# Taking ScalarE out of the row sums of six steps, and its align directive with it

## The chip, the cores and the metric

The kernel runs on one core of one Trainium2 chip. The metric is the device time of one execution in microseconds; for the kernel before, it is the median of three runs.

## The reference

For each of 8 batches, the reference multiplies a 4096x512 matrix `x` by the transpose of a 4096x512 matrix `y`, but keeps only the diagonal of the product, and takes a softmax over it. So only the row-by-row dot products of `x` and `y` are wanted:

```python
gram = np.matmul(x, y.transpose(0, 2, 1))        # B, N, D = 8, 4096, 512, all float32
diag = np.diagonal(gram, axis1=1, axis2=2)
diag = diag - diag.max(axis=-1, keepdims=True)
exp = np.exp(diag)
return (exp / exp.sum(axis=-1, keepdims=True)).astype(np.float32)
```

There are 32768 dot products of length 512. The inputs are 134.22 MB, the output is 0.13 MB.

## The kernel before, in words

TensorE is not used. The rows are laid over the 128 partitions, and each partition works through `R = 32` rows per step; there are eight steps, and four of them make one half of the output (four batches). One step takes in 8.39 MB of `x` and as much of `y`. There are two buffers for `x`, `xs[0]` and `xs[1]`, used in turn, and a single buffer `ys` for `y`. All loads are issued on one queue, that of SyncE (SP), in the order x, y, x, y.

The first six steps (t = 0 to 5) are the same, and are the ones that the change touches. VectorE (DVE) multiplies the first 26 rows of `xs` in place by `ys` (`products`, line 72). In the meantime ScalarE (ACT) copies the last `K = 6` rows of `ys` into a tile `side` (line 126), so that VectorE can multiply these rows from `side` and `ys` comes free earlier. As soon as both have read `ys`, SP issues the `y` load of the next step (line 68). Then the 512 products of each row are summed: VectorE reduces the first 30 rows in one instruction (`sums`, line 75), and ScalarE sums the last `W = 2` rows, each with an activation that has an accumulator as second output (`sums_act`, line 80). When both are done with this `xs` buffer, SP issues the `x` load of the step after the next into it (line 65). After the fourth step the softmax of the first half follows (`exps` and `normalize`, lines 93 to 113).

Step 6 and step 7 are written out differently. In step 6 ScalarE sums 30 rows, VectorE two. Step 7 loads in small pieces, and VectorE multiplies and sums each row in one instruction (`dots`, line 85), so that little is left to do after the last piece has landed. Then the softmax of the second half follows, and its result is stored from ScalarE's queue (line 169).

There is no scheduler: the order on each engine is that of the source, and the waits follow from which tile is read and written. Ahead of the loop stand one align directive for VectorE (line 117) and one for ScalarE (line 118). Such a directive asks that the next instruction of that engine be placed at a multiple of 128 instruction slots. In the trace each is one branch on its engine's queue, of 47 ns and 33 ns. Two drains of SP (lines 120 and 121) stand between them and the first load.

Of the kernel before, what the change touches and what calls it, by code (L numbers as in the profile page):

```python
# [1 line left out]

# [5 lines left out]


@with_exitstack
def kernel(
    ctx: ExitStack,
    tc: tile.TileContext,
    x: bass.AP,
    y: bass.AP,
    out: bass.AP,
):
    nc = tc.nc
    ctx.enter_context(tc.manual_schedule())  # L20
    f32 = mybir.dt.float32
    Alu = mybir.AluOpType
    Act = mybir.ActivationFunctionType
    X = mybir.AxisListType.X
    B, N, D = x.shape
    P = nc.NUM_PARTITIONS
    G = 32
    Q = P // G
    C = N // G
    R = 32  # L30
    H = R // 2
    K = 6
    W = 2
    F = H + 1
    L = 9
    S = B // Q * (C // R)


    xv = x.rearrange("(s b) (j c) d -> s (b j) c d", b=Q, j=G)
    yv = y.rearrange("(s b) (j c) d -> s (b j) c d", b=Q, j=G)  # L40
    ov = out.rearrange("(s b) (j c) -> s (b j) c", b=Q, j=G)

    big = ctx.enter_context(tc.tile_pool(name="big", bufs=1))
    small = ctx.enter_context(tc.tile_pool(name="small", bufs=1))


    xs = [big.tile([P, R, D], f32, name=f"xs{i}") for i in range(2)]
    ys = big.tile([P, R, D], f32, name="ys")
    side = big.tile([P, K, D], f32, name="side")

    diag = [small.tile([P, C + 2 * i], f32, name=f"diag{i}") for i in range(B // Q)]
    res = [small.tile([P, C], f32, name=f"res{i}") for i in range(B // Q)]

    def columns(t, r0, n):
        c0 = t % (C // R) * R + r0
        return slice(c0, c0 + n)

    def rows(t, r0, n):
        return xs[t % 2][:, r0 : r0 + n, :]

    def dots_of(t, r0, n):
        return diag[t * R // C][:, columns(t, r0, n)]

    def load_x(t, r0, n):
        nc.sync.dma_start(out=rows(t, r0, n), in_=xv[t * R // C, :, columns(t, r0, n), :])  # L65

    def load_y(t, r0, n):
        nc.sync.dma_start(out=ys[:, r0 : r0 + n, :], in_=yv[t * R // C, :, columns(t, r0, n), :])  # L68

    def products(t, r0, n, yt):  # L70
        xt = rows(t, r0, n)
        nc.vector.tensor_tensor(out=xt, in0=xt, in1=yt, op=Alu.mult)  # L72

    def sums(t, r0, n):
        nc.vector.tensor_reduce(out=dots_of(t, r0, n), in_=rows(t, r0, n), axis=X, op=Alu.add)  # L75

    def sums_act(t, r0, n):
        for r in range(r0, r0 + n):
            row = xs[t % 2][:, r, :]
            nc.scalar.activation(out=row, in_=row, func=Act.Copy, accum_out=dots_of(t, r, 1))  # L80

    def dots(t, r0, n):
        for r in range(r0, r0 + n):
            xt = xs[t % 2][:, r, :]
            nc.vector.scalar_tensor_tensor(  # L85
                out=xt, in0=xt, scalar=1.0, in1=ys[:, r, :], op0=Alu.mult, op1=Alu.mult,
                accum_out=dots_of(t, r, 1),
            )

    def over_quadrant(name, column, op, negate=False):  # L90

        got = small.tile([P, 1], f32, name=name)
        nc.vector.tensor_reduce(  # L93
            out=got, in_=column.to_broadcast([P, G]), axis=X, op=op, negate=negate, apply_transpose=True
        )
        return got

    def largest(out, d):
        nc.vector.tensor_reduce(out=out, in_=d, axis=X, op=Alu.max)  # L99

    def exps(i, d):
        mxp = small.tile([P, 1], f32, name=f"mxp{i}")
        largest(mxp, d)
        nmx = over_quadrant(f"nmx{i}", mxp, Alu.max, negate=True)
        sump = small.tile([P, 1], f32, name=f"sump{i}")
        nc.scalar.activation(out=res[i], in_=diag[i][:, :C], func=Act.Exp, bias=nmx, scale=1.0, accum_out=sump)  # L106
        return sump

    def normalize(i, sump):
        total = over_quadrant(f"sum{i}", sump, Alu.add)  # L110
        rc = small.tile([P, 1], f32, name=f"rc{i}")
        nc.vector.reciprocal(out=rc, in_=total)  # L112
        nc.vector.tensor_single_scalar(out=res[i], in_=res[i], scalar=rc, op=Alu.mult)  # L113

    nc.vector.addr_align(128, offset=0, max_nops=0)
    nc.scalar.addr_align(128, offset=0, max_nops=0)

    nc.sync.drain()  # L120
    nc.sync.drain()  # L121

    for t in range(S - 2):
        load_x(t, 0, R)
        load_y(t, 0, R)
        nc.scalar.activation(out=side, in_=ys[:, R - K :, :], func=Act.Copy)  # L126
        if t == C // R:
            normalize(0, sump)
        products(t, 0, R - K, ys[:, : R - K, :])
        products(t, R - K, K, side)  # L130
        sums(t, 0, R - W)
        sums_act(t, R - W, W)
        if t == C // R - 1:
            sump = exps(0, diag[0])

    t = S - 2
    load_x(t, 0, R)
    load_y(t, 0, R)
    spare = rows(t + 1, R - L, L)
    nc.scalar.activation(out=spare, in_=ys[:, F - L : F, :], func=Act.Copy)  # L140
    products(t, 0, F - L, ys[:, : F - L, :])
    products(t, F - L, L, spare)
    products(t, F, R - F, ys[:, F:, :])
    sums(t, R - W, W)
    sums_act(t, 0, R - W)
    largest(diag[1][:, C + 1 :], diag[1][:, : C - 2 * R])


    t += 1
    upto = {load_x: 0, load_y: 0}  # L150
    done = 0
    for load, n in (
        (load_x, H - 1), (load_y, F), (load_x, 8), (load_y, 10), (load_x, 6), (load_y, 3), (load_x, 2), (load_y, 2), (load_x, 1)
    ):
        load(t, upto[load], n)
        upto[load] += n
        both = min(upto.values())
        dots(t, done, both - done)
        done = both
        if done == F:  # L160
            largest(diag[1][:, C : C + 1], diag[1][:, C - 2 * R : C - R + H])

    met = small.tile([P, C - R], f32, name="met")
    nc.scalar.activation(out=met, in_=diag[1][:, : C - R], func=Act.Copy)  # L164

    for p in range(0, P, H):
        nc.sync.dma_start(out=ov[0, p : p + H, :], in_=res[0][p : p + H, :])
    normalize(1, exps(1, diag[1][:, C - R + H :]))
    nc.scalar.dma_start(out=ov[1], in_=res[1])


# [1 line left out]
_INS = ['x', 'y']  # L173
_OUTS = [((8, 4096), 'float32')]


# [23 lines left out]
```

## Time and profile before

| what | value |
|---|---|
| three runs | 320.30, 320.35, 320.43 us; median 320.35 |
| span of the profiled execution | 318.8 us |
| bytes read, mean rate over the span | 134.22 MB, 421 GB/s |
| VectorE busy | 241.7 us (76%), 98 instructions |
| ScalarE busy | 49.8 us (16%), 97 instructions |
| sum over 30 rows (line 75) | 6 of 16.153 us |
| sum over one row on ScalarE (line 80) | 42 of 0.617 us, and 42 reads of the accumulator of 0.187 us |

The page and the trace give the profiled execution its span, from the first to the last instruction, and no other time; the median of the runs is 1.55 us above that span. The busy share of an engine is over the whole span; whether an engine's work sets the end is read from the chain of waits and from the idle time ahead of its instructions.

### The profile page before, as it was taken

Reading aid. Unit: us, or ns where it says so; the run is one execution under the profiler, and the core shown is the slowest. Engines: PE = TensorE matmul, PEld = TensorE weight load, DVE = VectorE, ACT = ScalarE, POOL = GpSimd, SP = SyncE. Lnnn points to the kernel's source line nnn. Section 1 sums busy time; section 2 is a strip of 40 time slices with the busy share of each in tenths; the row PEclk is TensorE's granted clock in tenths of the full one; section 3 lists DMA queues with packets and bytes.
Section 4 is the critical chain, followed back from the end, with each engine's and each line's share of the span. In section 5 each row is a group of like instructions: output and inputs, shape, how many; then the busy total and the mean of one; then the engine's idle time right before and its main releaser. Section 6 shows DMA issues by size and latency. Waiting matters only on the chain.

```text
span 318.8 us, 315 instructions
## 1 busy us (share of the span) xinstructions
DVE 241.7 (76%) x98; ACT 49.8 (16%) x97; POOL 0.2 (0%) x4
## 2 busy tenths in 40 slices
DVE  0000069995899939999399994999939998599996
ACT  1000030100301003010120103000030100596700
POOL 0000000000000000000000000000000000000000
DMA  9999999999999999999999999999999999999993
GB/s 372 419 395 469 452 395 452 469 395 395 493 428 395 469 452 395 428 477 411 395 485 436 395 469 452 395 403 493 419 395 469 452 395 452 394 440 410 429 411 112
DMA packets 3714, 134.37 MB, mean 421 GB/s; under 512 B 512, under 2 KB 768, under 8 KB 1280
## 3 DMA queue, kind: packets, MB, share of 16 engines
q1 hardware_dynamic: 3568, 134.29, 97.7%
q10 hardware_dynamic: 144, 0.07, 0.1%
q14 instruction: 2, 0.02, 0.0%
HBM read 134.22 MB, written 0.13 MB: 421 GB/s over the span
## 4 chain that ended last, share of the span: by engine, by line
DMA 65%; DVE 33%; SPq 1%; issue 0%; ACT 0%; DVEq 0%
DMA ys<-in_y_dram 65%; DVE xs L72 32%; DVE xs L85 0%; SPq L65 0%; SPq L68 0%; DVE res L113 0%; DVE sum L93 0%; DVE nmx L93 0%; ACT res L106 0%; DVE mxp L99 0%; DVE rc L112 0%; DVEq L72 0%; SPq L121 0%; SPq L120 0%
## 5 line engine op out<-in xcount | busy, mean ns | idle before, releaser
L72 DVE TENSOR_TENSOR xs<-xs,ys 128x13312 f32<-128x13312 f32 (+2 forms) x8 | 96.7, 12091 | 71.9 <-DMA ys<-in_y_dram 71.9
L75 DVE TENSOR_REDUCE diag<-xs 128x30 f32<-128x15360 f32 (+1 forms) x7 | 98.1, 14020 | 0.2
L80 ACT ACTIVATE xs<-xs 128x512 f32<-128x512 f32 x42 | 25.9, 617 | 90.4 <-DVE xs L72 90.4
L126 ACT ACTIVATE side<-ys 128x3072 f32<-128x3072 f32 x6 | 16.6, 2763 | 124.1 <-DMA ys<-in_y_dram 124.1
L85 DVE SCALAR_TENSOR_TENSOR xs<-xs,ys 128x512 f32<-128x512 f32 x32 | 19.9, 687 | 1.1 <-DMA ys<-in_y_dram 1.0
L72 DVE TENSOR_TENSOR xs<-xs,side 128x3072 f32<-128x3072 f32 x6 | 20.1, 3351 | 0.0
L80 ACT ACTIVATION_READ_ACCUMULATOR xs<-xs 128x1 f32 x42 | 7.9, 187 | 0.0
L140 ACT ACTIVATE xs<-ys 128x4608 f32<-128x4608 f32 x1 | 4.0, 4043 | 20.0 <-DMA ys<-in_y_dram 20.0
L106 ACT ACTIVATE res<-diag,nmx 128x128 f32<-128x128 f32 x2 | 0.8, 402 | 30.1 <-DVE nmx L93 30.1
L72 DVE TENSOR_TENSOR xs<-xs,xs 128x4608 f32<-128x4608 f32 x1 | 5.0, 4951 | 0.0
L85 DVE DVE_READ_ACCUMULATOR xs<-xs,ys 128x1 f32 x32 | 2.6, 82 | 0.0
L126 ACT ACT_TABLE_LOAD x1 | 1.3, 1283 | 1.2 <-PEq L184 1.2
L93 DVE TRANSPOSE_TENSOR_REDUCE sum<-sump 128x1 f32<-128x32 f32 x2 | 0.4, 212 | 1.2 <-ACT res L106 1.2
L113 DVE TENSOR_SCALAR res<-res,rc 128x128 f32<-128x128 f32 x2 | 0.6, 286 | 0.1
L99 DVE TENSOR_REDUCE mxp<-diag 128x1 f32<-128x128 f32 (+1 forms) x2 | 0.5, 229 | 0.1
L93 DVE TRANSPOSE_TENSOR_REDUCE nmx<-mxp 128x1 f32<-128x32 f32 x2 | 0.4, 211 | 0.1
L99 DVE TENSOR_REDUCE diag<-diag 128x1 f32<-128x64 f32 (+1 forms) x2 | 0.4, 202 | 0.0
L112 DVE RECIPROCAL rc<-sum 128x1 f32<-128x1 f32 x2 | 0.3, 164 | 0.1
L106 ACT ACTIVATION_READ_ACCUMULATOR res<-diag,nmx 128x1 f32 x2 | 0.4, 186 | 0.0
L164 ACT ACTIVATE met<-diag 128x96 f32<-128x96 f32 x1 | 0.3, 283 | 0.0
L184 POOL MEMSET const-bfloat16-1.0<- 128x1 bf16 x1 | 0.1, 102 | 0.0
L184 POOL MEMSET const-uint8-127<- 128x1 uint8 x1 | 0.1, 101 | 0.0
(2 smaller groups left out, 0.2 us busy)
## 6 DMA issues: line engine op xcount, KB each, us to landing
ys<-in_y_dram SPq DMA_DIRECT2D x1, 4352.0 KB, 14.9
xs<-in_x_dram SPq DMA_DIRECT2D x1, 3840.0 KB, 14.2
ys<-in_y_dram SPq DMA_DIRECT2D x1, 2560.0 KB, 12.9
xs<-in_x_dram SPq DMA_DIRECT2D x1, 2048.0 KB, 19.4
xs<-in_x_dram SPq DMA_DIRECT2D x1, 1536.0 KB, 16.3
ys<-in_y_dram SPq DMA_DIRECT2D x1, 768.0 KB, 17.7
xs<-in_x_dram SPq DMA_DIRECT2D x1, 512.0 KB, 18.5
ys<-in_y_dram SPq DMA_DIRECT2D x1, 512.0 KB, 19.3
```

Of the source, the lines that this page charges most:

```text
L72: nc.vector.tensor_tensor(out=xt, in0=xt, in1=yt, op=Alu.mult)
L75: nc.vector.tensor_reduce(out=dots_of(t, r0, n), in_=rows(t, r0, n), axis=X, op=Alu.add)
L80: nc.scalar.activation(out=row, in_=row, func=Act.Copy, accum_out=dots_of(t, r, 1))
L85: nc.vector.scalar_tensor_tensor(out=xt, in0=xt, scalar=1.0, in1=ys[:, r, :], op0=Alu.mult, op1=Alu.mult, accum_out=dots_of(t, r, 1),)
L93: nc.vector.tensor_reduce(out=got, in_=column.to_broadcast([P, G]), axis=X, op=op, negate=negate, apply_transpose=True)
L99: nc.vector.tensor_reduce(out=out, in_=d, axis=X, op=Alu.max)
L106: nc.scalar.activation(out=res[i], in_=diag[i][:, :C], func=Act.Exp, bias=nmx, scale=1.0, accum_out=sump)
L112: nc.vector.reciprocal(out=rc, in_=total)
L113: nc.vector.tensor_single_scalar(out=res[i], in_=res[i], scalar=rc, op=Alu.mult)
L126: nc.scalar.activation(out=side, in_=ys[:, R - K :, :], func=Act.Copy)
L140: nc.scalar.activation(out=spare, in_=ys[:, F - L : F, :], func=Act.Copy)
L164: nc.scalar.activation(out=met, in_=diag[1][:, : C - R], func=Act.Copy)
```

## The change

The align directive of ScalarE (line 118) is taken out; that of VectorE stays. In the six like steps VectorE's reduction takes all 32 rows, and ScalarE's twelve activations with accumulator are gone. `W` is still used in step 6, which is not touched. The wait of five of the `x` loads on ScalarE goes with the activations; their wait on VectorE stays. All lines from 118 on move up by one, those from 131 on by two.

```diff
     nc.vector.addr_align(128, offset=0, max_nops=0)
-    nc.scalar.addr_align(128, offset=0, max_nops=0)
...
         products(t, R - K, K, side)
-        sums(t, 0, R - W)
-        sums_act(t, R - W, W)
+        sums(t, 0, R)
         if t == C // R - 1:
             sump = exps(0, diag[0])
```

## The prediction

> **What bounds the kernel now.** I read the page's slices first, because a kernel that only streams its inputs should show its DMA engines full.
>
> ```profile
> DVE  0000069995899939999399994999939998599996
> ACT  1000030100301003010120103000030100596700
> DMA  9999999999999999999999999999999999999993
> ```
>
> Each digit is a fortieth of the span. The DMA row is at 90% or more from the first slice to the last but one. VectorE has holes in every step, ScalarE is mostly idle. So something that ends earlier or later on VectorE or ScalarE moves the end only if it makes a hole in the DMA row, or if it lies after the last landing.
>
> Second, the chain that ended last, in order of time, for the pitch of the steps:
>
> ```profile
> 56.62 24.50 DMA ys<-in_y_dram
> 81.12 0.03 issue
> ...
> 81.21 14.04 DVE xs L72
> 95.25 0.02 SPq L68
> 95.27 0.03 issue
> 95.30 24.52 DMA ys<-in_y_dram
> ```
>
> The columns are start, length and what. The chain names VectorE's product and the y load in turn, but that is not a VectorE bound: 24.5 us is issue to landing of a load whose bytes take less, since it first queues behind the x load ahead of it. The y loads land at 81.12 and 119.82, 38.70 us apart, and in each interval 16.78 MB come in: 433.5 GB/s. At that rate one load takes 19.35 us. All 134.22 MB need 309.6 us of the 318.8; the rest is the start (the first load is issued at 0.83) and the tail after the last landings (313.24 to 318.8).
>
> Third, the groups of instructions with shapes kept apart, for the prices:
>
> ```profile
> L75 DVE TENSOR_REDUCE diag<-xs 128x30 f32<-128x15360 f32 x6 | 96.9, 16153 | 0.2
> L72 DVE TENSOR_TENSOR xs<-xs,ys 128x13312 f32<-128x13312 f32 x6 | 84.2, 14025 | 66.7 <-DMA ys<-in_y_dram 66.7
> L75 DVE TENSOR_REDUCE diag<-xs 128x2 f32<-128x1024 f32 x1 | 1.2, 1220 | 0.0
> ```
>
> The last columns are busy us, mean ns of one, and idle time of the engine before them with what ended it. The product always waits for y: 42.5 us once at the start, then about 5 us per step.
>
> Fourth, the timeline, for how early the x loads are issued:
>
> ```profile
> 59.83 16.15 DVE L75 TENSOR_REDUCE diag<-xs 128x30 f32<-128x15360 f32 x1
> 60.98 0.19 ACT L80 ACTIVATION_READ_ACCUMULATOR xs<-xs 128x1 f32 x1
> 76.06 0.33 SPq L65 DMA_DIRECT2D xs<-in_x_dram  x1
> 81.21 14.03 DVE L72 TENSOR_TENSOR xs<-xs,ys 128x13312 f32<-128x13312 f32 x1 [5.22 <-DMA ys<-in_y_dram]
> ```
>
> The x load of step 2 goes out at 76.06, right after the reduction (75.98); ScalarE had finished at 61.17. The y load then in flight lands at 81.12. So the next load is in the queue 5.06 us before the one ahead of it has landed. This lead is what the change eats into.
>
> **The change part by part.**
>
> *The longer reduction.* From 1,024 elements (1.220 us) to 15,360 (16.153 us) the slope is 14.933 us over 14,336 elements, 1.042 ns each. Two more rows are 1,024 elements, so +1.067 us: 17.22 us. Six of them are 6.4 us of VectorE time. In a step VectorE then works from 81.21 to about 115.76 instead of 114.69, and its idle time before the next product falls from 5.22 to about 4.15 us. In step 3 the softmax of the first half also follows; its idle time was 3.24 us by the timeline and becomes about 2.2. Idle time remains in every step, so the product still starts on the landing of y, and the y load after it is issued when it was. Cost while this cover holds: 0. Without it: up to 1.07 us a step.
>
> *The later x loads.* Six x loads (steps 2 to 7) are released by these reductions. Each is issued 1.07 us later, at 77.13 for the first, and the lead shrinks from 5.06 to 3.99 us. How much lead is needed the trace does not state, so I bound it. The first load is issued at 0.83, and the DMA share is 0.53 in the window 0 to 2 us and 0.97 in 2 to 4 us: the engines are filled within about 2.5 us of an issue. And the y load of step 7 is issued at 279.27, while the x load ahead of it, issued at 269.63, lands after 14.2 us at 283.8: a lead of 4.6 us that leaves no hole in the DMA row. 3.99 is above 2.5 and a little below 4.6, so it lies outside the leads seen in steady running, but above the need seen at the start. Lower bound 0, upper bound six times 1.07 or 6.4 us; I take 0, by the row at the start, which is the nearest to what is asked (issue to full engines). SP has nothing else to lose: the instruction after the delayed x load is the next y load, which waits for a product that ends 19 us later.
>
> *The removed activations.* Twelve activations of 0.617 us and twelve accumulator reads of 0.187 us. A pair of rows occupies ScalarE from 59.83 to 61.17, 1.34 us, beside a reduction of 16.15 us. Nothing waits for them that does not wait longer for the reduction. ScalarE's next work is the copy at 81.20. Gain: 0. No transfer is removed or added, and steps 6 and 7 and the last softmax are as before, so the tail (313.24 to 318.8) keeps its length.
>
> *The removed directive.* It is one branch of 33 ns at 0.73 us; after it ScalarE loads its table at 1.17 and then waits for y until 42.43. Up to 0.4 us may be saved there under a wait of 40 us: 0. Two other things hang on it. In the stretch from 1 to 3 us the trace has instruction fetches, and nowhere else in the span:
>
> ```profile
> q14 instruction: 2, 0.02, 4.8%
> ```
>
> That is packets, MB and share of 16 engines: two packets of about 8 KB, and 4.8% of 16 engines over 2 us is 1.54 us of DMA engine time, 0.77 us each. They follow the two branches of lines 117 and 118 by about a microsecond. Without ScalarE's branch, one of them should either vanish or be fetched later, when ScalarE's code runs over the next boundary. If it goes, one of 16 DMA engines has up to 0.77 us less to do; the loads land when the slowest engine is done, so the gain is between 0 and 0.77 us. If it comes in mid-run, the same bounds hold as a loss against a start without it, so between a loss of 0.77 and a gain of 0.77 in all. I take 0, because only one engine of 16 is concerned and the window from 2 to 4 us has the others still filling.
>
> The Trainium skill (Runtime: NRT & Kernel Launch, Instruction fetch mechanics) says that an engine's code is fetched ahead in order, block by block, so that running over a boundary is mostly hidden, while a taken branch out of the fetched window stalls the engine. It calls a block 16 KiB; the packets here are of 8 KB. By that rule too the sum would be 0 for the boundary, and a small gain on ScalarE for the branch, under the same 40 us wait.
>
> Sum against the profiled execution: 318.8 + 0, and 1.55 us around it as in the runs before: 320.35 us.
>
> **The rivals.**
>
> *A: all hidden,* as summed: 320.35, give or take 0.3 for small shifts in the landings. For it: full DMA row, 4 us of VectorE idle time left, 40 us of cover for ScalarE. Against it: the lead and the fetch are bounded, not measured.
>
> *B: ScalarE's code is fetched in mid-run (slower).* Place: where ScalarE's unaligned code reaches a boundary, a packet goes between full data queues. Price: 0.77 us if it lands on the DMA engine that finishes last, and 0.40 us more if ScalarE stalls there just before the last exponential (the idle time seen after its branch, 0.77 to 1.17 us). So 320.65 to 321.5. It decides once the packet costs the last engine over 0.64 us. Against it: ScalarE counts 97 instructions before and 73 after, so there is less code to run over a boundary, and most of it has cover.
>
> *C: the lead is too short (slower).* If a load needs more than 3.99 us to fill the engines without a hole, each of six x loads opens one, of up to 1.07 us: 320.35 to 326.8. It decides from a needed lead of about 4.0 us. Against it: 2.5 us sufficed at the start. The Trainium skill (VectorE: DVE Perf Modes, Rules for kernel authors) warns of this direction: it calls the reduction VectorE's slowest operation and advises against it on the hot path. The trace disagrees in part: 1.052 ns per element here against 1.054 for the product.
>
> *D: a lighter start (faster).* One fetch fewer lets the last engine begin and end earlier: down to 320.35 - 0.77, or 319.6.
>
> That the change does not do what it says I can exclude for the sums (the built program has reductions of 32 rows and no such activations); for the directive, the branch in the trace shows that it was more than a remark.
>
> **How the numbers follow.** A measurement of this kernel can tell 0.2%, or 0.64 us, from no change. A has 0.76; B 0.12, of which 0.08 is over 0.64 us; C 0.05; D 0.07, of which 0.05 is over 0.64 us. Faster 0.05; slower 0.08 + 0.05 = 0.13; same 0.82. The range takes in A and most of B and D, and leaves out C and the far ends: 319.9 to 321.1.
>
> **What would show it.** Right: reductions of 17.2 us; the first delayed x load at about 77.1; y landings still 38.7 us apart (81.1, 119.8); VectorE idle about 4.1 us before the product; one instruction packet or two, wherever they lie; a span of 318.5 to 319.1. Wrong by C: a pitch of 39 us or more and lower digits in the DMA row. Wrong by B: an instruction packet after 3 us and the same pitch otherwise, with later last landings. Wrong by D: all landings early by the same part of a microsecond from the first on. A different length of the tail after the last landing would be something I have not seen.

## The result, and the profile after

The changed kernel takes 320.84 us (median of 13 runs, 320.41 to 322.53), the kernel before 320.43 us (13 runs, 320.30 to 320.85). The ratio is 1.0017, with a 95% interval of 1.0009 to 1.0025: the change makes the kernel slower, by 0.41 us between the medians and by 0.3 to 0.8 us by the interval. That is inside the range that the prediction gave and less than the 0.2% below which it called the time the same, but it is more than the uncertainty of the comparison, and the forecast was that nothing moves.

The profiled execution of the changed kernel has a span of 318.9 us, against 318.8; the spans of single executions differ by tenths from each other, so below the profiles are used for where time goes, and the medians of the runs for how much. The timeline, start and length first:

```profile
59.76 17.22 DVE L75 TENSOR_REDUCE diag<-xs 128x32 f32<-128x16384 f32 x1
77.01 0.33 SPq L65 DMA_DIRECT2D xs<-in_x_dram  x1
...
81.14 14.03 DVE L72 TENSOR_TENSOR xs<-xs,ys 128x13312 f32<-128x13312 f32 x1 [4.15 <-DMA ys<-in_y_dram]
```

The reduction, the x issue and VectorE's idle time are those of the prediction's sum (17.22, 77.1 and 4.15 us). VectorE is nowhere the bound. The chain that ended last, start, length and what:

```profile
56.55 24.50 DMA ys<-in_y_dram
81.04 0.03 issue
...
95.22 24.62 DMA ys<-in_y_dram
119.84 0.03 issue
...
134.03 24.67 DMA ys<-in_y_dram
158.70 0.03 issue
```

Here is the difference. The y landings are 38.80 and 38.86 us apart (81.04, 119.84, 158.70) where they were 38.70 us apart before, and a y load takes 24.62 and 24.67 us from issue to landing where it took 24.5. VectorE's products keep their 14.04 us. So the loads themselves lose a little, just behind the two x loads issued at 77.01 and 115.71. The next three y loads are back at 24.50 to 24.53 us.

The trace lists every packet. Before, of the 64 KB packets that start within 6.5 us of an x issue, 2, 0, 6, 0, 0 and 0 took longer than 2.43 us in the six steps; after the change 18, 12, 9, 2, 0 and 0 did. The usual length is 2.42 us; those over 2.5 us in the first two of these steps start 2.6 to 3.4 us after the issue and take up to 2.83 us. They end after the y load has landed, so they belong to the x load, and they are among its first. Eight of them start between 79.65 and 80.45 us, where the last 16 packets of the y load end one after another (79.65 to 80.56), half a microsecond and more before that load has landed (81.04). That they run on the engines that are through with y first is thus near at hand; the trace does not say which engine moved a packet.

The other difference is the instruction fetch (packets, MB, share of 16 engines), first in the stretch from 1 to 3 us, then from 270 us to the end:

```profile
q14 instruction: 1, 0.01, 2.7%
```

```profile
q14 instruction: 1, 0.01, 0.0%
```

One of the two packets has left the start. It is now fetched at 288.9 us, while ScalarE is in the sums of step 6.

### The profile page after: what moved, and what is told of

The parts are those of the page before. It is cut to its first block, busy times and chain, and to the rows that moved or that the text cites. A ratio compares the mean times of both kernels' runs of the same rounds, so it can differ in the third digit from the quotient of the medians.

```text
span 318.9 us, 283 instructions
## 1 busy us (share of the span) xinstructions
DVE 248.0 (78%) x98; ACT 41.8 (13%) x73; POOL 0.2 (0%) x4
## 4 chain that ended last, share of the span: by engine, by line
DMA 65%; DVE 33%; SPq 1%; issue 0%; ACT 0%; DVEq 0%
DMA ys<-in_y_dram 65%; DVE xs L72 32%; DVE xs L85 0%; SPq L65 0%; SPq L68 0%; DVE res L113 0%; DVE nmx L93 0%; DVE sum L93 0%; ACT res L106 0%; DVE mxp L99 0%; DVE rc L112 0%; DVEq L72 0%; SPq L120 0%; SPq L119 0%
## 5 line engine op out<-in xcount | busy, mean ns | idle before, releaser
L75 DVE TENSOR_REDUCE diag<-xs 128x32 f32<-128x16384 f32 (+1 forms) x7 | 104.5, 14934 | 0.2
L80 ACT ACTIVATE xs<-xs 128x512 f32<-128x512 f32 x30 | 18.4, 616 | 2.8 <-DVE xs L72 2.8
L80 ACT ACTIVATION_READ_ACCUMULATOR xs<-xs 128x1 f32 x30 | 5.6, 188 | 0.0
## 6 DMA issues: line engine op xcount, KB each, us to landing
xs<-in_x_dram SPq DMA_DIRECT2D x1, 1536.0 KB, 16.3
```

## The experiments

Three theories were set against each other. **L**: the x loads are issued too late; 4.0 us before the load ahead has landed is not enough, and their first packets run slow. **F**: ScalarE's code, no longer aligned, has a packet fetched in mid-run, and that holds up a DMA engine. The third, named in the expectations where it matters, is that VectorE's longer work, or ScalarE's missing share, costs time by itself. Each kernel below was timed against the kernel before on the same chip.

**Each half of the change alone.** The first has ScalarE's directive put back into the changed kernel:

```diff
     nc.vector.addr_align(128, offset=0, max_nops=0)
+    nc.scalar.addr_align(128, offset=0, max_nops=0)
```

> The changed kernel with ScalarE's align directive put back; VectorE still sums all 32 rows. Theory L (the x loads are issued too late, so that their first packets run slow): as slow as the changed kernel, 0.3 to 0.6 us over the kernel before, and slow packets of 2.5 to 2.8 us about 3 us after the x issues. Theory F (ScalarE's code, unaligned, is fetched in mid-run and that costs the time): equal to the kernel before within 0.15 us, with both instruction packets before 3 us.

Measured: 320.86 against 320.44 us, ratio 1.0013 (1.0004 to 1.0021). The sums alone make the kernel slower. Both code packets are back at the start, and the chain shows a loss at the same place, behind an x load:

```profile
95.05 25.05 DMA ys<-in_y_dram
120.10 0.03 issue
```

The other half is the kernel before without ScalarE's directive:

```diff
     nc.vector.addr_align(128, offset=0, max_nops=0)
-    nc.scalar.addr_align(128, offset=0, max_nops=0)
```

> The kernel before with only ScalarE's align directive taken out; the sums stay shared, 30 rows and 2. Theory L: equal to the kernel before within 0.15 us, x issues at 76.06 and few slow packets, though one instruction packet moves from the start into mid-run. Theory F: 0.3 to 0.6 us slower than the kernel before.

Measured: 320.62 against 320.44 us, ratio 1.0005 (0.9996 to 1.0013). By itself this is inconclusive: it allows nothing, and it allows 0.4 us. Its profile has a code packet at 279.5 us, and the last y load takes 19.62 us from issue to landing in place of 19.27; the six steps take as long as before to 0.1 us.

**Late issue without any more work on VectorE.** ScalarE touches the x buffer once more after VectorE's reduction, so that only the release is later:

```diff
         sums_act(t, R - W, W)
+        both = rows(t, 0, 2)
+        nc.scalar.activation(out=both, in_=both, func=Act.Copy)
```

> The kernel before (VectorE sums 30 rows, ScalarE 2, aligned), and ScalarE then copies the first two rows of the x buffer onto themselves, which waits for VectorE's reduction and holds the x buffer about 1.1 us longer. VectorE does exactly what it did before; only the x issue moves, to about 77.2. Theory L (late issue): as the changed kernel, 0.3 to 0.6 us slower than the kernel before, with slow packets 2.5 to 4 us after the x issues. If the longer reduction itself slowed the loads: no difference within 0.15 us.

Measured: 320.94 against 320.42 us, ratio 1.0014 (1.0005 to 1.0022). The timeline and the chain:

```profile
75.83 1.06 ACT L134 ACTIVATE xs<-xs 128x1024 f32<-128x1024 f32 x1 [14.85 <-DVE diag L75]
76.91 0.33 SPq L65 DMA_DIRECT2D xs<-in_x_dram  x1
...
81.02 14.03 DVE L72 TENSOR_TENSOR xs<-xs,ys 128x13312 f32<-128x13312 f32 x1 [5.22 <-DMA ys<-in_y_dram]
```

```profile
95.11 24.65 DMA ys<-in_y_dram
119.76 0.03 issue
...
133.94 24.72 DMA ys<-in_y_dram
```

VectorE reduces 30 rows and idles 5.22 us, as before the change; the x issue is where the changed kernel has it, and the y loads take 24.65 and 24.72 us, as there. VectorE's longer work is therefore not what costs the time: the late issue is, here with no code packet in mid-run either.

**More and less of it.** The first two sum two or four rows a second time before the buffer is released:

```diff
+    def again(t, n):
+        nc.vector.tensor_reduce(out=spill[:, :n], in_=rows(t, 0, n), axis=X, op=Alu.add)
...
         sums(t, 0, R)
+        again(t, 2)
```

> As align_back, and VectorE sums two rows of each of the six steps a second time, into a scratch tile, before the x buffer is released: about 1.22 us more VectorE work, x issues at about 78.2, a lead of about 2.8 us in place of 4.0 and 5.06. VectorE still has about 2.9 us of idle time a step. Theory L: much worse than the changed kernel, 1.5 to 5 us over the kernel before, and growing per step. Theory F: no difference from the kernel before. If VectorE's work as such slowed the loads and not their late issue, the loss would only double, to about 0.8 us.

> As extra2, with four rows summed a second time: lead about 2 us, VectorE's idle time before the next product still about 2 us. Theory L: every x load opens a hole, more than 6 us slower than before: 8 to 14 us. If the loss in extra2 came from something that saturates: 6 us again.

Measured: 326.43 against 320.44 us with two rows (ratio 1.0203, 1.0182 to 1.0225), 328.87 against 320.42 with four (1.0243, 1.0203 to 1.0283). About 1.1 us less lead than in the changed kernel makes a loss of 6 us out of one of 0.4. The next 1.08 us cost about 2.5 more by the medians, but the two intervals overlap and the executions spread over 3 and 5 us, so this second step is not well measured. Of extra2:

```profile
77.91 0.33 SPq L65 DMA_DIRECT2D xs<-in_x_dram  x1
...
80.92 14.03 DVE L72 TENSOR_TENSOR xs<-xs,ys 128x13312 f32<-128x13312 f32 x1 [3.04 <-DMA ys<-in_y_dram]
...
116.62 0.33 SPq L65 DMA_DIRECT2D xs<-in_x_dram  x1
...
121.11 14.02 DVE L72 TENSOR_TENSOR xs<-xs,ys 128x13312 f32<-128x13312 f32 x1 [4.51 <-DMA ys<-in_y_dram]
```

The lead is 2.9 us and the product behind it starts 40.19 us after the one before (80.92, 121.11). VectorE still idles 3.04 and 4.51 us: it stays far from being the bound while the kernel loses 6 us. In the packets there are now gaps besides long ones: between 79 and 81 us packets are underway for 0.89 of the 16 engines' time, against 1.00 in the changed kernel. An x load that loses time makes the y load behind it land later, while the next x issue goes by VectorE's clock: so it has more lead (2.9, 4.4, 3.0, 3.4, 3.8 and 4.1 us in the six steps). That would explain why the loss does not grow in proportion.

In the other direction, one row and six rows on ScalarE (`W` in the six steps replaced by 1 and by 6):

> The kernel before with ScalarE summing one row of each of the six steps, VectorE 31: lead about 4.5 us, between the kernel before (5.06) and the changed one (4.0). Theory L: between the two, 0.1 to 0.4 us slower than before. If there were a sharp point between 4.0 and 4.5 us: no difference within 0.15 us.

> The kernel before, aligned, with ScalarE summing 6 rows of each of the six steps in place of 2, VectorE 26. The reduction is 4.17 us shorter, x issues at about 71.9, a lead of about 9.2 us. Theory L: no slow packets after x issues; 0 to 0.2 us faster than the kernel before. Theory F: ScalarE's code grows by 48 instructions past a boundary of 128 slots, so a packet is fetched in mid-run: 0.3 to 0.6 us slower than before.

Measured: w1 320.45 against 320.42 us, ratio 1.0001 (0.9993 to 1.0010). No loss is seen, where theory L expected 0.1 to 0.4 us; this is the expectation's sharp point. By the medians a lead of 4.54 us is as good as one of 5.06, and the loss sets in between 4.04 and 4.54 us; the interval still allows 0.3 us for w1. Of w1, a steady chain:

```profile
95.20 24.53 DMA ys<-in_y_dram
119.73 0.03 issue
```

w6: 320.65 against 320.44 us, ratio 1.0009 (1.0000 to 1.0017). The expected lead of 9.2 us was reckoned wrongly (four rows are 2.13 us, not 4.17): it is 7.3 us. Behind the x issues the packets lose 0.005 us an engine at most, but there is nothing to gain either, and by its median the kernel loses 0.2 us. ScalarE's code is longer by 48 instructions, a third code packet is fetched at 287.9 us, and the last y load takes 19.52 us in place of 19.27.

**Halving the loads.** Three kernels split loads into two of 16 rows (the y loads of the six steps, or the x loads of steps 2 to 6), to see whether the lead is needed as time or as packets, and to release half of x earlier:

```diff
-        load_y(t, 0, R)                     # after_ysplit
+        load_y(t, 0, H)
+        load_y(t, H, H)
...
-        load_x(t, 0, R)                     # xsplit_aligned, after_xsplit
+        load_x(t, 0, R if t < 2 else H)
+        if t >= 2:
+            load_x(t, H, H)
...
-        sums(t, 0, R)
+        sums(t, 0, H)
+        sums(t, H, H)
```

> The changed kernel with each y load of the six steps issued as two loads of 16 rows, one right behind the other: same bytes and same lead in time (about 4 us), but the y packets are of 32 KB in place of 64 KB, so twice as many are queued ahead of the x load. If the lead is needed as time: as slow as the changed kernel, 0.3 to 0.6 us over the kernel before. If it is needed as a number of packets queued: back to the kernel before within 0.2 us, few slow packets.

> VectorE sums all 32 rows of the six steps, as in the changed kernel, ScalarE's align directive is back, and each of these sums is two instructions of 16 rows; from step 2 on the x load of a step is two loads of 16 rows, so the first is issued after the first half of the sum, at about 68.5 us in place of 77.0, some 12 us before the y load ahead of it has landed; the second follows at about 77.1, while the first half of x has still to be moved. Theory L: equal to the kernel before within 0.2 us, or up to 0.2 us faster, and no slow packets after the x issues. If the cause were VectorE's longer work or ScalarE's missing one: 0.3 to 0.6 us slower, as the changed kernel.

> The same without ScalarE's align directive, that is the changed kernel with the sums and the x loads of the six steps in halves. With the late issue out of the way, the directive alone is left: theory L: as xsplit_aligned within 0.15 us; theory F: 0.2 to 0.6 us slower than xsplit_aligned, from the instruction packet in mid-run.

Measured: after_ysplit 321.33 against 320.42 us (1.0029, 1.0018 to 1.0040), xsplit_aligned 320.87 against 320.37 (1.0015, 1.0006 to 1.0024), after_xsplit 321.31 against 320.37 (1.0028, 1.0016 to 1.0039). None is back at the time of the kernel before, where theory L expected xsplit_aligned within 0.2 us of it, and after_ysplit is slower than either of its two expectations. So a control followed, the kernel before with halves, which has a long lead anyway:

> The kernel before (VectorE 30 rows, ScalarE 2, aligned) with the sums and the x loads of the six steps in halves, as in xsplit_aligned: a control on what the halving itself costs. If halving costs the time (80 packets of 32 KB an engine, 1.213 us each in the trace against half of 2.420): as xsplit_aligned, 0.3 to 0.6 us slower than before, though the lead is long. If the halving is free and VectorE's 32 rows were what cost xsplit_aligned its time: equal to the kernel before within 0.15 us.

Measured: 321.24 against 320.41 us, ratio 1.0029 (1.0019 to 1.0038). Halving costs 0.8 us even where ScalarE sums its two rows and no load is late. Not all of it is in the loads. The record has the span of every execution beside its time, and the time outside the span is 1.78 us on average in the kernel before and within 0.04 us of that in most kernels, but 2.05 us in xsplit_shared. Inside the span xsplit_shared is 0.6 us longer than the kernel before, and xsplit_aligned 0.5. The half loads' packets take 1.213 us (median in xsplit_aligned) against half of 2.420; 80 of them an engine are 0.24 us, so that is part of it, and the rest is not accounted for. As remedies for the late issue these kernels therefore decide nothing; the ysplit question, time or packets, stays open.

One comparison among them does bear on theory F. The kernel after_xsplit is xsplit_aligned without ScalarE's directive, timed on the same chip, and it is 0.44 us slower between the medians, as F expected (0.2 to 0.6); all six of its executions lie above the median of the other. Its code packet comes at 288.6 us, and its last y load takes 19.51 us against 19.27 in xsplit_aligned.

**The lead restored without ScalarE.** VectorE can multiply and sum a row in one instruction (line 85, a row every 0.61 us), which for the rows from `side` saves the reduction. With all six:

```diff
-        products(t, R - K, K, side)
-        sums(t, 0, R)
+        dots(t, R - K, K, side)             # in1 is side's row in place of ys's
+        sums(t, 0, R - K)
```

> The changed kernel (no row sums on ScalarE in the six steps, its align directive back) with the six rows that come from the side tile multiplied and summed by VectorE in one instruction each, as step 7 does, and the other 26 reduced. One x load, packets as before. VectorE's work after the product falls from 3.35 + 17.22 to about 3.7 + 14.0 us, so the x issue comes at about 74.2 and the lead is 6.8 us with VectorE alone. Theory L: equal to the kernel before within 0.2 us, no slow packets after the x issues. If ScalarE's missing share itself were the cause: 0.3 to 0.6 us slower.

Measured: 321.14 against 320.41 us, ratio 1.0021 (1.0012 to 1.0030). Missed. But the loss is not in the six steps: with a lead of 6.95 us their pitch is 38.70 us throughout, and the chain is 0.30 us ahead of the kernel before when the y of step 6 lands (274.39 against 274.69). It is in step 7:

```profile
274.48 17.38 DVE xs L72 x3
...
293.67 20.25 DMA ys<-in_y_dram
313.94 1.34 DVE xs L86 x4
```

The last y load takes 20.25 us from issue to landing, 19.27 before. VectorE's code is longer here, and a code packet is fetched at 299.0 us. That reopened theory F. With only the last row fused both code packets are fetched before 3 us:

```diff
-        products(t, R - K, K, side)
-        sums(t, 0, R)
+        products(t, R - K, K - 1, side[:, : K - 1, :])
+        dots(t, R - 1, 1, side[:, K - 1 :, :])
+        sums(t, 0, R - 1)
```

> The changed kernel with ScalarE's directive back, and the last row of each of the six steps multiplied and summed by VectorE in one instruction; 31 rows reduced. ScalarE sums nothing in the six steps. VectorE's work shrinks by about 0.45 us against the changed kernel, lead about 4.5 us as in w1, and VectorE's code (125 slots by the program) stays within 128. Theory L: equal to before within 0.2 us (as w1). If ScalarE's missing share or VectorE's longer work were the cause: 0.3 to 0.6 us slower.

Measured: 320.54 against 320.35 us, ratio 1.0006 (0.9998 to 1.0015): no loss that can be told from none. The spans of its executions are those of the kernel before (318.65 us on average, both); the 0.19 us lie outside the span (1.92 against 1.78 us). ScalarE sums nothing in the six steps here, and a lead of 4.61 us is enough.

**The code packet alone.** Two kernels are the kernel before with one number changed, the slot at which VectorE's or ScalarE's code begins:

```diff
-    nc.vector.addr_align(128, offset=0, max_nops=0)
+    nc.vector.addr_align(128, offset=72, max_nops=0)    # off_dve
...
-    nc.scalar.addr_align(128, offset=0, max_nops=0)
+    nc.scalar.addr_align(128, offset=64, max_nops=0)    # off_act
```

> The kernel before, with VectorE's align directive given an offset of 72 slots in place of 0, and nothing else changed: VectorE's code then runs over a 128-slot boundary in step 7, near 299 us, as it did in fused_side. Theory F (a code packet fetched between the last loads holds up one DMA engine): slower than before by 0.2 to 0.9 us, with the landing times of step 7 lengthened from that point, x issues and lead unchanged. Theory L alone: equal to before within 0.15 us.

> The kernel before, with ScalarE's align directive given an offset of 64 slots: its code runs over the boundary in step 6, near 285 us, as that of the changed kernel and align_out does. Theory F: slower than before by 0.1 to 0.4 us, as align_out was in its one profile (landings of step 7 about 0.3 us longer). Theory L alone: equal to before within 0.15 us.

Measured: off_dve 320.86 against 320.35 us, ratio 1.0014 (1.0006 to 1.0023); off_act 320.76 against 320.35, ratio 1.0014 (1.0005 to 1.0023). The instructions of the computation and their order are the same, and both are slower by 0.4 to 0.5 us. The DMA issues of step 7 (size, and us from issue to landing) show where; before, then off_dve, with its packet at 298.6 us:

```profile
ys<-in_y_dram SPq DMA_DIRECT2D x1, 2560.0 KB, 12.9
xs<-in_x_dram SPq DMA_DIRECT2D x1, 2048.0 KB, 19.4
xs<-in_x_dram SPq DMA_DIRECT2D x1, 1536.0 KB, 16.3
```

```profile
q14 instruction: 1, 0.01, 0.0%
...
ys<-in_y_dram SPq DMA_DIRECT2D x1, 2560.0 KB, 13.4
xs<-in_x_dram SPq DMA_DIRECT2D x1, 2048.0 KB, 19.4
xs<-in_x_dram SPq DMA_DIRECT2D x1, 1536.0 KB, 16.8
```

The x piece of 2048 KB, landing at about 298.8, is as before; all that land behind the code packet are 0.5 us late. In off_act the packet comes at 282.8 and the last y load takes 19.45 in place of 19.27 us, which is less than half of the 0.41 us. ScalarE itself does not stop: its sums go on every 0.61 us through the boundary.

The last kernel is fused_side with VectorE's code at slot 72, so that the packet comes earlier:

> fused_side with VectorE's directive at an offset of 72 slots, so that its code runs over the boundary in step 3, in the middle of the large loads, in place of 299 us. Lead 7 us. Theory F, with the place of the packet deciding its price: less than fused_side's 0.7 us, 0 to 0.4 us over the kernel before. If the 0.7 us of fused_side came from something else than the packet at 299 us: again 0.5 to 0.9 us.

Measured: 321.14 against 320.35 us, ratio 1.0026 (1.0017 to 1.0036). Missed. Its profile shows the packet at 164.4 us, one y load 0.23 us longer than its neighbours, and a step 7 as before:

```profile
133.81 24.52 DMA ys<-in_y_dram
...
172.51 24.75 DMA ys<-in_y_dram
...
211.45 24.53 DMA ys<-in_y_dram
```

So the loss of fused_side in step 7 went with the packet: the last y load takes 19.27 us again. The time did not follow, and the packet's 0.2 us are only a part of the 0.8. Of the rest, 0.37 us lie outside the span (2.15 against 1.78 us in the kernel before), which the trace does not cover; what is left, about 0.2 us, the profiled execution does not show.

## Why the prediction was wrong

The stretch from the product of step 1 to that of step 6 (five intervals of the timeline, so without the start and without step 7) sets the kernels with a short lead apart from the others. Each figure is from one profiled execution:

| kernel | usual lead of the x issues, us | step 1 to step 6, us | time over before, us |
|---|---|---|---|
| fused_side | 6.95 | 193.50 | +0.73 (code packet in step 7) |
| kernel before | 5.06 | 193.57 | |
| fused_one | 4.61 | 193.50 | +0.19, not told from none, outside the span |
| w1 | 4.54 | 193.52 | +0.03, not told from none |
| changed kernel | 4.04 | 193.76 | +0.41 |
| act_late | 4.02 | 193.84 | +0.52 |
| align_back | 4.04 | 194.16 | +0.42 |
| extra2 | 2.9 to 4.4 | 197.67 | +5.99 |
| extra4 | 1.8 to 4.7 | 200.21 | +8.45 |

A tenth or two in this column does not tell two kernels apart: align_out, off_dve and w6, with leads of 5.06 us and more, have 193.65 to 193.67. That the late issue costs time rests on the medians of the changed kernel, align_back and act_late, and on the size of the loss in extra2 and extra4.

*The longer reduction.* Right in every number: +1.07 us, 17.22 us, idle time 4.15 us, 2.28 in step 3 (predicted 2.2), and no cost of its own, as act_late shows from the other side.

*The later x loads.* This is the step that failed. The bound of 2.5 us was read from the start of the kernel as "engines filled", from the busy share alone. The window view that it came from has a rate beside the share:

```profile
2.00:4.00 2.00, 0.00 (x0) 0.45 (x1) 0.00 (x0) 1.00 0.97 360
20.00:40.00 20.00, 0.00 (x0) 0.00 (x0) 0.00 (x0) 1.00 1.00 433
```

The last two columns are DMA share and GB/s. The view puts a packet, with its whole length and all its bytes, into the stretch in which it starts. In a stretch of 2 us, where packets of 64 KB take longer than that, neither column is what the engines did: the 360 GB/s are eleven such packets. Their ratio can be read, and it is 371 GB/s for full engines in place of 433. The packets themselves say it better. The first 16 start 1.0 to 2.5 us after the first issue, so 2.5 us is right as the time by which all have begun; but they take 2.4 to 3.2 us in place of 2.42. The engines are filled by then, and not yet at their rate, and a busy engine with a slow packet counts as busy. Nor is the lead to the landing the time that a load has: the last y packets end 0.5 to 1.4 us before the landing, so 4.03 us of lead were 2.64 us until the first engine was free (77.01 to 79.65). Against the 2.5 us that leaves almost no margin, and with extra2's 2.9 us of lead there are gaps. Slow first packets come back in mid-run when a load is issued too shortly before its turn. Between the two rows that the prediction weighed, it took the one "nearest to what is asked"; the other, the 4.6 us of step 7 (4.53 by the landing in the trace), was a lead in steady running with no loss, and the point found lies between 4.04 and 4.54 us, just under it. A term taken as 0 should have been a few tenths of a microsecond: +0.42 us in align_back and +0.52 in act_late by the medians (0.07 of the latter outside the span), about 0.2 to 0.6 us in the six steps by the profiles. The chance of 0.82 for "same" also rested on 0.64 us as the least that can be told from no change; with 13 runs of each kernel the interval is 0.5 us wide. The 1.55 us that the sum puts around the span set the profiled execution against the median of three; the time outside the span of one and the same execution is 1.73 to 1.83 us in the kernel before. Since the sum starts and ends at the measured median, this changes nothing in it.

*Rival C* was thus the right mechanism, with a chance of 0.05, and mis-sized: it opened holes of up to 1.07 us at once, where the loss begins softly (long packets on some engines) and hits some steps and not others: in the changed kernel the leads of 4.02 to 4.04 us in the last three of the six steps cost nothing that shows, and why is open. The digits of the DMA row, named as its sign, did not change: a long packet is a busy one.

*The removed directive.* Taken as 0, too. The packet did move into mid-run, as said, and off_dve and off_act show that such a packet costs 0.4 to 0.5 us, after_xsplit against xsplit_aligned 0.44; rival B had up to 0.77 for it, and what is late in their profiles is what it named, the last landings. The rule of the Trainium skill (Runtime: NRT & Kernel Launch, Instruction fetch mechanics) that a boundary is mostly hidden holds for the engine that runs the code, which does not stop (0.61 us a row through the boundary in off_act), but not for a kernel whose loads fill all DMA engines: off_act is 0.41 us slower than the kernel before.

*The removed activations.* Right: nothing waited for them. ScalarE's share mattered only through the row of VectorE work that it took off the lead; fused_one does without it.

*What stays open.* The changed kernel has both causes, and each alone costs about as much as both (align_back +0.42, off_act +0.41, changed kernel +0.41 us). They do not add up. In the changed kernel's profile the pieces of step 7 land as before (2560 KB after 13.0, 1536 KB after 16.3 us, the last y load after 19.30), so there the packet at 289 us cost nothing to be seen. It is the exception: in the five other kernels with such a packet at 279 to 289 us the last y load takes 19.45 to 19.62 us. A load lands after the last of its packets (before the change, the last 16 of the y load end between 79.73 and 80.67 us, and it lands at 81.12), so two delays on different engines can hide each other; that they do so here is an argument, not shown. The late issue is enough to explain the time; the share of the directive in it is not known. By itself the directive costs between none and 0.4 us by align_out's interval, and 0.44 us between the two kernels with halved x loads. None of the sixteen kernels beats the kernel before.

## What to carry to other kernels

In a kernel that keeps all DMA engines full, slack has to be measured at the issue of the next load, not at the engine that frees its buffer: here VectorE had 4 us to spare and a microsecond of them still cost time. Read the rate beside the busy share, over a stretch of many packets, since a slow packet looks busy, and bound a lead by rows of steady running. When a change moves code across a boundary, look for the instruction packet in mid-run as one more transfer on a full queue.

## What was not expected of the hardware

The first packets of a load that is issued about 4 us before its turn took up to 2.99 us in the changed kernel in place of 2.42, and not in every step, though the engines had other packets to work on until then; with 4.54 us (w1) the longest took 2.57. A code packet of 8 KB, 0.31 to 0.33 us long in mid-run, made the last y load 0.5 us longer in off_dve, 0.2 in off_act and 1.0 in fused_side (20.25 against 19.27 us). And two loads of 4 MB were not as good as one of 8 MB: five x loads in halves made the span 0.5 us longer in xsplit_aligned and 0.6 in xsplit_shared.
